# A hybrid decoder block on one core: the convolution branch's projection by seven quarter products instead of eight, with block sums of its operands kept in DRAM

## The chip, the cores and the metric

One core of a Trainium2 chip runs the whole kernel. The time is device microseconds of one execution; a kernel's time is the median of several. The kernel before has 1921.81 us (three runs, 1920.85 to 1922.24).

## The reference, cut to what matters

One layer, 2048 tokens, 1024 channels, everything in float32. The change concerns `y_a`, and the order of work around it.

```python
h = rms_norm(x, norm_g)
u = jnp.einsum('bsd,dc->bsc', h, w_in)
v_c, b_c, c_c, z_c, q, k, v, z_a, gate_logits = jnp.split(u, SPLIT_POINTS, axis=-1)

y_c = b_c * causal_depthwise_conv(c_c * v_c, conv_w)
y_c = y_c * jax.nn.silu(z_c)
y_a = jnp.einsum('bsc,cd->bsd', y_c, w_conv_out)
...
o = sliding_window_attention(q, k, v, sinks) * jax.nn.silu(z_a)
y_b = jnp.einsum('bsc,cd->bsd', o, w_attn_out)

gates = jax.nn.sigmoid(gate_logits + gate_b)
g_a, g_b = jnp.split(gates, N_BRANCHES, axis=-1)
merged = g_a * y_a + g_b * y_b
return x + jnp.einsum('bsd,de->bse', merged, w_out)
```

## The kernel before

**Tiling.** The tokens are worked on in two sets of T = 1024 (`t` = 0 and 1). A projection is computed in *units*: 256 output columns (two blocks of 128, index `i`) by the 1024 tokens of the set (two halves of H = 512, index `q`). The reduction over 1024 channels has 8 chunks of 128 (KC = 8), as 4 pairs (KP = 4): a pair index `j` and a parity `p`. Each float32 product is made of three matmuls of rounded parts: high by high, high by low, low by high. So a chunk takes 3 matmuls, and a plain unit 4 quarters x 8 chunks x 3 = 96 matmuls of 128x512.

**Seven quarter products.** `sunit` (L443 to L476) computes a unit by a scheme of the Strassen and Winograd kind: output blocks `i` and token halves `q` are the quarters of the result, parities `p` those of the reduction, and seven products of quarter size (`product`, L426) on sums and differences of quarters take the place of eight. A product is 4 chunks x 3 = 12 matmuls, a unit 84. Operands are numbered 1 to 8: 1, 2, 8 and 3 are the raw quarters, 5, 6, 7 and 4 sums of them; `op_split` makes the high part (ScalarE) and the low part (VectorE) of one. The weights' sums are made per unit: one by an accumulating DMA on GpSimd's queue (`added`, L269), three by VectorE (L363). `qunit` (L478) computes a unit by plain products from the raw quarters alone.

**Order.** `run` (L623) drives everything by a clock of products: at each tick (12 matmuls) it takes one step of the unit's generator, issues weight loads ahead (`ahead_loads`), one piece of weight preparation (`piece`, L387), and what was `put` to that tick. So the order on each engine's queue is written out by hand in ticks. Per set: q, conv and gate units, z units of the convolution branch (`z`) and of attention (`za`), then four `yb` units (attention's projection), then four `ya` units (the convolution's projection); after both sets eight `o` units. In the second set k, v come first, then one `ga` unit at its place after them. Attention's blocks are put to a list of ticks between the units.

**The stage that is changed.** The gated convolution is written to DRAM (`ocd`) in the z stage. During `yb` it is read back in 16 tiles of 128x512 a set (`load`, names `ocr`), split by `split_op` into `opa`, and `ya_unit` (L1248) computes its units by `branch` and `mm_t` (L1167), 8 chunks for each of 4 quarters. The result is multiplied by the gate (read back from `gd` into one of two buffers of `upool`, named `tha`, L1256) and accumulated into `mt` in DRAM by GpSimd's queue (L1262); `yb`'s results have been written to `mt` before. During `ya`, `next_tile` (L1568) reads the second set's rows of x (whole rows, 512 KB) and columns of x transposed (`h`) on ScalarE's queue, computes the norm and makes the operands of the next set; after the second set `wo_side` (L1287) does the like for `w_out`. Weights for `ya` are laid out by the host in another form (`branch` in `_layout`, kind "T" in `pieces_of`): two halves of 4 chunks each.

Of the kernel before, what the change touches and what calls it, by code (L numbers as in the profile page):

```python
# [15 lines left out]
P = 128  # L16
# [40 lines left out]
EARLY = (1, 0)  # L57
# [6 lines left out]
def block_kernel(  # L64
# [56 lines left out]
    yd = [dram.tile([KC, P, T], F32, name=f"yd{t}") for t in range(NT)]  # L121
    mt = [dram.tile([KC, P, T], F32, name=f"mt{t}") for t in range(NT)]
# [153 lines left out]
    def load_half(i=None):  # L276
# [12 lines left out]
        if kind == "R":  # L289
            raw = both[:, h]  # L290
            for p in range(2):
                nc.sync.dma_start(raw[:, p], srcs[(2 * h + p) * P : (2 * h + p + 1) * P])

                for c in FIRST_X.get((i, p), ()):
                    xt_load(c, 0)
        elif kind in "SP":
            raw = both.rearrange("p k h (j c) -> p k h j c", c=P)
            for k in range(2) if key[0] == "o" else (slice(0, 2),):
                nc.sync.dma_start(raw[:, k, h], block_of(n, h, k))
            if kind == "S" and h:  # L300
                put(tick[0] + ADDED, lambda: added(n))
        else:
            raw = both[:, h].rearrange("p k (j c) -> p (k j) c", c=UC)
            w, c0 = srcs
            nc.sync.dma_start(raw, w[c0 // UC, h].rearrange("r (j c) -> r j c", c=UC))
# [12 lines left out]
    def pieces_of(n):  # L318
# [52 lines left out]
        def part(p):  # L371
            hi, lo = (v.rearrange("p (j c) -> p j c", c=UC) for v in wpair(f"{name}_{p}"))
            w[p] = (hi, lo)
            return two(hi, lo, raws[2 * n + p])

        return w, [(2, 0, lambda: part(0)), (2, 2, lambda: part(1))]
# [10 lines left out]
    def piece():  # L387
# [4 lines left out]
        need = [2 * n + i] if plan[n][0] in "TP" else [2 * n, 2 * n + 1][: 1 + min(i, 1)]  # L392
# [717 lines left out]
    def fin_g(t, w, j):  # L1110
        def fin(i, q, val):
            k = 2 * j + i
            th = slot([P, H], F32, f"th{t}_{w}_{k}_{q}")
# [45 lines left out]
    def split_op(src, name):  # L1159
        o = optile(name)  # L1160
        split(o[:, 0], o[:, 1], src)
        return o


    YA_CHUNKS = (0, 2, 4, 6, 1, 3, 5, 7)

    def mm_t(ps, u, half, opt, q, last):  # L1167
        cs = slice(half * P, (half + 1) * P)
        for n, k in enumerate(YA_CHUNKS):
            j, p = divmod(k, 2)  # L1170
            force(u, p)
            hi, lo = ready[u][p]
            o = opt[k, q]
            for i, (w, m) in enumerate(((hi, 0), (hi, 1), (lo, 0))):
                nc.tensor.matmul(  # L1175
                    ps, lhsT=w[:, j, cs], rhs=o[:, m, :],
                    start=n == 0 and i == 0, stop=n == KC - 1 and i == 2)
            if n == KP - 1:
                live[0] -= 2 * last
                yield  # L1180
        live[0] -= 2 * last

    def quarters(order):
        return [(hf, q) for q in order for hf in range(2)]

    def branch(t, key, j, opt, fin, order):
        u = unit((key, t, j))
        for n, (hf, q) in enumerate(quarters(order)):
            ps = bank(f"{key}{t}_{j}_{hf}_{q}")
            yield from mm_t(ps, u, hf, opt, q, n == 3)  # L1190
            fin(2 * j + hf, q, ps)
            yield

    def load(src, k, q, name):
        tl = slot([P, H], F32, name)
        nc.sync.dma_start(tl, src[k, :, hs(q)])
        return tl

# [27 lines left out]
    def yb_unit(t, j, ops):  # L1226
        th = {}
        order = ((0, 1), (1, 1), (0, 0), (1, 0)) if j == 0 else ((0, 0), (1, 1), (0, 1), (1, 0))

        def get(n):  # L1230
            pair = upool.tile([P, 2 * H + 2], F32, tag="u", name=f"thb{t}_{j}_{n}")
            for e, (i, q) in enumerate(order[2 * n : 2 * n + 2]):
                th[i, q] = pair[:, hs(e)]
                nc.sync.dma_start(th[i, q], gd[t][1][2 * j + i, :, hs(q)])

        def fin(i, q, val):
# [7 lines left out]
            nc.sync.dma_start(mt[t][2 * j + i, :, hs(q)], m)  # L1244

        return yb_first(t, ops, fin) if j == 0 else sunit(("yb", t, j), ops, fin), get

    def ya_unit(t, j, opt, order):  # L1248
        th = {}

        def get(n):
            pair = upool.tile([P, 2 * H + 2], F32, tag="u", name=f"tha{t}_{j}_{n}")
            for i, (hf, q) in enumerate(quarters(order)[2 * n : 2 * n + 2]):
                k = 2 * j + hf
                th[k, q] = pair[:, hs(i)]
                nc.sync.dma_start(th[k, q], gd[t][0][k, :, hs(q)])  # L1256

        def fin(k, q, ps):
            m = th[k, q]
            vec.scalar_tensor_tensor(  # L1260
                out=m, in0=m, scalar=1.0, in1=ps, op0=ALU.add, op1=ALU.mult)
            nc.gpsimd.dma_start(mt[t][k, :, hs(q)], m, accum_op=ALU.add)  # L1262

        return branch(t, "ya", j, opt, fin, order), get
# [3 lines left out]
    def fin_o(n):  # L1268
# [4 lines left out]

        def get(i, q):
            xr = xrs[i, q] = slot([P, H], F32, f"xr{n}_{i}_{q}")
# [11 lines left out]
    def wo_side(n0, st):  # L1287
        raw = st["raw"]

        def ld(c):  # L1290
            for q in range(2):
                h = raw[c, q] = slot([P, H], F32, f"wo_{c}_{q}")
                nc.scalar.dma_start(h, w_o[c * P : (c + 1) * P, hs(q)])

        def sums(j):
            a, b = 2 * j, 2 * j + 1
            sub(raw[a, 1], raw[b, 1], raw[a, 1])
            sub(raw[a, 0], raw[b, 1], raw[a, 0])

        for j in range(KP):  # L1300
            for i in range(2):
                put(n0 + 2 * j + i, lambda c=2 * j + i: ld(c))
            put(n0 + 6 + 2 * j, lambda j=j: form(2, 1, j, st))
            put(n0 + 7 + 2 * j, lambda j=j: sub(raw[2 * j, 0], raw[2 * j, 1], raw[2 * j, 0]))
            put(n0 + 8 + 2 * j, lambda j=j: form(2, 5, j, st))
            put(n0 + 9 + 2 * j, lambda j=j: sums(j))
            put(n0 + 17 + j, lambda j=j: form(2, 6, j, st))
            put(n0 + 28 + j, lambda j=j: form(2, 2, j, st))
            put(n0 + 30 + j, lambda j=j: form(2, 7, j, st))
            put(n0 + 22 + j, lambda j=j: last_sum(j, st))  # L1310
            put(n0 + 32 + j // 2, lambda j=j: form(2, 3, j, st))
            put(n0 + 34 + j // 2, lambda j=j: form(2, 4, j, st))
# [3 lines left out]
    for t in range(NT):  # L1316
# [9 lines left out]
        else:  # L1326
            at_(("k", t), COL_K)
            at_(("v", t), COL_VV)
        for j in range(EARLY[t]):
# [16 lines left out]
        for j in range(NJ):  # L1346
            plan.append(("T", (w_co, j * UC), ("ya", t, j)))
    for n in range(S // P // 2):
        t, c0 = divmod(2 * n * P, T)
        s(("o", n), (mt[t], c0), (mt[t], c0 + P))  # L1350

# [216 lines left out]
    def next_tile(t, n0):  # L1568

        st = x_state(t)  # L1570
        raw, ops, xs = st["raw"], st["ops"], st["x"]

        def ld(b):
            xs[b] = x_load(t, b, nc.scalar)

        def stats(b0):
            ss = st["ss"][b0] = small.tile([P, 2], F32, tag="sx", bufs=4, name=f"ss{t}_{b0}")
# [187 lines left out]
```

## Time and profile before

| | |
|---|---|
| median of 3 runs | 1921.81 us (1920.85 to 1922.24) |
| profiled execution | 1922.65 us, its span 1920.9 us |
| granted TensorE clock | 1.000 |
| matmuls | 8774, of these 7894 of 128x512 |
| TensorE / VectorE / ScalarE / GpSimd busy | 1908.7 / 1454.0 / 973.0 / 606.9 us |
| data moved | 378.87 MB, 197 GB/s on average |
| `ya` stage of the first set | about 804.7 to 892 us |
| `ya` stage of the second set | 1677.5 to 1764.5 us |

The profile is of one execution; its times start with the span. In a group of instructions, `out<-in` gives the program's names, then the shape, the count after x, and after the bar the busy time, the mean time of one in ns, and the idle time of the engine ahead of them. SPq and POOLq are the queues of the engines that issue DMAs. In the waits, the name to the right of the arrow is what ended the wait.

### The profile page before, as it was taken

The page shows a single profiled execution, that of the slowest core. Times are in us where ns is not written, and L with a number is a line of the kernel's source. Part 1 is how long each engine was busy: PE and PEld are TensorE (multiplying, and loading weights), DVE is VectorE, ACT ScalarE, POOL GpSimd, SP SyncE. Part 2 cuts the span into 40 slices and gives each one's busy share as a digit, 9 for nine tenths or more (in the row PEclk, how much of TensorE's full clock was granted, in tenths as well). Part 3 has the DMA queues.
Part 4 walks back from the last instruction along what each step waited for, and adds up shares of the span by engine and source line. Part 5 has one row for each costly group of instructions (what it writes and reads, how often), then busy time and mean ns, then how long its engine had stood idle before and what let it go on. Part 6 is the DMA issues. An engine that isn't in the chain of part 4 may idle for free.

```text
span 1920.9 us, 27491 instructions
## 1 busy us (share of the span) xinstructions
PE 1908.7 (99%) x8774; PEld 1589.1 (83%) x8774; DVE 1454.0 (76%) x2501; ACT 973.0 (51%) x1935; POOL 606.9 (32%) x833
## 2 busy tenths in 40 slices
PE   8999999999999999999999999999999999999999
PEld 7888888888888888888888888888888888888887
DVE  7988888888777659668688888878888458755544
ACT  7555455456666344334565554556666335423221
POOL 2043435446564100011432444546665000011000
PEclk9999999999999999999999999999999999999999
DMA  8298556668887544894696665678887624886663
GB/s 298 86 238 211 168 168 185 181 195 257 243 267 236 171 121 152 297 285 104 165 229 172 186 174 157 179 232 243 245 256 228 200 98 144 271 233 137 175 191 110
DMA packets 278928, 378.87 MB, mean 197 GB/s; under 512 B 62784, under 2 KB 141632, under 8 KB 278784
## 3 DMA queue, kind: packets, MB, share of 16 engines
q1 hardware_dynamic: 233216, 280.57, 46.5%
q0 software_dynamic: 39664, 83.92, 19.8%
q10 hardware_dynamic: 5904, 12.62, 2.0%
q8 instruction: 70, 1.15, 0.3%
q14 instruction: 74, 0.61, 0.1%
HBM read 263.49 MB, written 113.51 MB: 196 GB/s over the span
## 4 chain that ended last, share of the span: by engine, by line
PE 96%; DMA 2%; DVE 1%; ACT 0%; POOL 0%; issue 0%; SPq 0%; DVEq 0%; POOLq 0%; ACTq 0%
PE Y L432 33%; PE ya L1175 9%; PE Vcv L432 5%; PE Xcv L432 4%; PE po L1037 2%; PE Vgb L432 2%; PE Xgb L432 2%; PE Xz L432 2%; PE Vo L432 2%; PE Xo L432 2%; PE Vza L432 2%; PE Xza L432 2%; PE yb L1216 2%; PE Vb L432 2%; PE Vz L432 2%; PE Xb L432 2%
## 5 line engine op out<-in xcount | busy, mean ns | idle before, releaser
L999 POOL DMA_DIRECT2D x<-fd x256 | 141.4, 565 | 116.1 <-DMA fd<-f 68.0
L972 ACT ACTIVATE p<-s,st,rq 128x128 f32<-128x128 f32 x256 | 113.0, 451 | 0.8 <-DMA fd<-f 0.6
L1020 POOL TENSOR_SCALAR_AFFINE_SELECT xh<-xh 64x512 fp32r<-64x512 f32 x64 | 64.7, 1011 | 106.2 <-DVE xl L214 79.6
L1262 POOL DMA_DIRECT2D mt<-tha x32 | 27.8, 881 | 217.3 <-DVE tha L214 195.3
L992 POOL DMA_DIRECT2D fd<-f x64 | 39.6, 618 | 152.4 <-DVE f L214 135.4
L432 PE MATMUL Xcv<-oph,wcv_ah 128*128 128x512 f32 x256 | 79.2, 390 | 0.0
L1175 PE MATMUL ya<-opa,wya_0h 128*128 128x512 f32 x256 | 79.0, 390 | 0.0
L1175 PE MATMUL ya<-opa,wya_1h 128*128 128x512 f32 x256 | 78.8, 389 | 0.0
L214 DVE SCALAR_TENSOR_TENSOR tha<-tha,ya 128x512 f32<-128x512 f32 x32 | 22.0, 686 | 61.1 <-PE ya L1175 55.8
L1020 POOL TENSOR_SCALAR_AFFINE_SELECT xl<-xl 64x512 fp32r<-64x512 f32 x64 | 60.5, 946 | 4.4
L1020 POOL TENSOR_SCALAR_AFFINE_SELECT yp<-yp 64x512 fp32r<-64x512 f32 x64 | 58.8, 919 | 4.2
L1020 POOL TENSOR_SCALAR_AFFINE_SELECT yp<-xl 64x512 fp32r<-64x512 f32 x64 | 57.8, 904 | 3.1
L214 DVE TENSOR_TENSOR o<-po,o 64x256 f32<-64x256 f32 x128 | 53.5, 418 | 5.2 <-ACT o L1049 4.3
L1175 PEld LDWEIGHTS ya<-opa,wya_1h 128*128 128x128 f32 x256 | 48.0, 188 | 9.9
L1175 PEld LDWEIGHTS ya<-opa,wya_0h 128*128 128x128 f32 x256 | 47.9, 188 | 9.9
L432 PEld LDWEIGHTS Xcv<-oph,wcv_ah 128*128 128x128 f32 x256 | 47.6, 188 | 9.6
L274 POOL DMA_DIRECT2D wyb_raw<-in_w_attn_out x6 | 5.1, 842 | 156.3 <-DMA wyb_raw<-in_w_attn_out 74.5
L214 DVE SCALAR_TENSOR_TENSOR y<-u,cols,y 128x512 f32<-128x512 f32 x64 | 49.9, 779 | 3.5 <-ACT y L1086 2.3
L1049 ACT COPY o<-po 64x256 f32<-64x256 f32 x128 | 47.1, 368 | 10.1 <-PE po L1037 4.7
L972 ACT ACTIVATION_READ_ACCUMULATOR p<-s,st,rq 128x1 f32 x256 | 50.9, 199 | 0.0
L214 DVE TENSOR_TENSOR p<-p,st 128x512 f32<-128x512 f32 x64 | 48.1, 752 | 3.4 <-DMA q<-q2d 0.3
L214 DVE TENSOR_TENSOR ophc<-zain,ophc 128x512 fp32r<-128x512 f32 x64 | 42.2, 686 | 11.1 <-ACT ophc L241 11.1
(628 smaller groups left out, 6384.0 us busy)
## 6 DMA issues: line engine op xcount, KB each, us to landing
gd<-th SPq DMA_DIRECT2D x64, 256.0 KB, 3.3
wcv_raw<-in_w_in SPq DMA_DIRECT2D x32, 512.0 KB, 5.3
q<-q2d SPq DMA_DIRECT2D x64, 256.0 KB, 5.3
v<-vd SPq DMA_DIRECT2D x128, 128.0 KB, 4.0
fd<-f POOLq DMA_DIRECT2D x64, 256.0 KB, 4.6
x<-fd POOLq DMA_DIRECT2D x256, 64.0 KB, 3.7
wga_raw<-in_w_in SPq DMA_DIRECT2D x16, 512.0 KB, 5.6
wq_raw<-in_w_in SPq DMA_DIRECT2D x16, 512.0 KB, 6.0
```

What stands on the lines that cost most here:

```text
L214: r = f(*args, **kw)
L274: nc.gpsimd.dma_start(raw[:, 0, 1], block_of(n, 1, 1), accum_op=ALU.add)
L432: nc.tensor.matmul(ps, lhsT=w[:, j, :], rhs=b[:, m, :], start=start and j == 0 and i == 0, stop=j == KP - 1 and i == 2, skip_group_check=n ...
L972: nc.scalar.activation(out=p[:, i, :], in_=sg[:, i, HD : 3 * HD], func=AF.Exp, bias=st[:, 1, i : i + 1], scale=rv[:, i // 2, i % 2 : i % 2 ...
L992: nc.gpsimd.dma_start(fd, f)
L999: nc.gpsimd.dma_start(x[QUADS[k]], src[k])
L1020: nc.gpsimd.affine_select(out=d4, in_=s4, pattern=[[0, 2], [-32 * sg, 2], [0, G], [-sg, 32]], compare_op=ALU.is_gt if prev else ALU.is_ge, ...
L1037: nc.tensor.matmul(po[:, cs], lhsT=v2[:, kind, :], rhs=xx[:, :, h * HD : (h + 1) * HD], start=n == 0, stop=n == 2)
L1049: nc.scalar.copy(ov, pov[oth, :, e])
L1175: nc.tensor.matmul(ps, lhsT=w[:, j, cs], rhs=o[:, m, :], start=n == 0 and i == 0, stop=n == KC - 1 and i == 2)
L1216: nc.tensor.matmul(banks[i, q], lhsT=w[:, j, :], rhs=b[:, l, :], start=n == 0 and m == 0, stop=n == KC - 1 and m == 2, skip_group_check=True)
L1262: nc.gpsimd.dma_start(mt[t][k, :, hs(q)], m, accum_op=ALU.add)
```

## The change

1. **`ya` by seven products.** `y_unit` replaces `yb_unit` and `ya_unit`. The first unit of each set's `ya` is plain (`qunit`), the other three are `sunit`s. `w_conv_out` is laid out as the other weights are, so the "T" form, `mm_t`, `branch`, `load` and `split_op` go. Gate halves and the accumulation into `mt` stay as they were.
2. **Block sums by way of DRAM.** In the last `z` unit of the convolution branch `csum` reads the four quarters of `ocd` per pair `j` into slots (16 loads a set), makes four differences on VectorE, and writes them to a DRAM tensor `csd`. The operands of `ya` (32 a set, instead of 16) are read by `conv_op` from `ocd` (raw quarters) or `csd` (sums), three ticks ahead of the split, at ticks of a table (`CONV_AT`).
3. **First units plain.** The second set runs its first two `ga` units ahead of k and v, the first of them plain; the first `o` unit is plain.
4. **Queues and places.** The columns `h`, the rows of x (now as halves of 256 KB, 16 loads) and `w_out` are loaded by SP instead of ScalarE's queue, and from the `yb` stage on; the squares work on 512 columns at a time. Attention's ticks, and those of the next set's operands, are given by tables. Attention of the second set ends later, in the z stage.

Instructions before and after: matmuls 8774 and 8726; DMAs issued by SP 1264 and 1408, by ScalarE 41 and 1, by GpSimd 563 and 567; activation table loads 8 and 10.

```diff
-EARLY = (1, 0)
+EARLY = (1, 2)
+CSUM_AT = ((3, 3, 11, 15), (1, 6, 13, 12))
+CONV_AT = ((5, 2, 4, 3, 6, 2, 5, 6, 6, 6, 5, 6, 7, 7, 12, 12, 12, 12, 11, 13, 14, 14, 14, 16, 15, 17, 12, 16, 17, 19, 20, 19), (3, 1, 1, 1, 1, 1, 4, 7, 5, 4, 8, 6, 8, 8, 7, 9, 12, 12, 13, 14, 14, 15, 15, 10, 14, 16, 18, 18, 19, 20, 19, 17))
...
+    csd = [dram.tile([4, KP, P, H], F32, name=f"csd{t}") for t in range(NT)]
...
-        nc.scalar.dma_start(h, xt2[c * P : (c + 1) * P, t * T + q * H : t * T + (q + 1) * H])
+        nc.sync.dma_start(h, xt2[c * P : (c + 1) * P, t * T + q * H : t * T + (q + 1) * H])
...
-    def yb_unit(t, j, ops):
+    def y_unit(t, w, j, ops):
...
-            nc.sync.dma_start(mt[t][2 * j + i, :, hs(q)], m)
-
-        return yb_first(t, ops, fin) if j == 0 else sunit(("yb", t, j), ops, fin), get
-
-    def ya_unit(t, j, opt, order):
...
-        return branch(t, "ya", j, opt, fin, order), get
+            to = mt[t][2 * j + i, :, hs(q)]
+            if w:
+                nc.sync.dma_start(to, m)
+            else:
+                nc.gpsimd.dma_start(to, m, accum_op=ALU.add)
+
+        if j:
+            return sunit(key, ops, fin), get
+        return (yb_first(t, ops, fin) if w else qunit(key, ops, fin)), get
...
-            plan.append(("T", (w_co, j * UC), ("ya", t, j)))
+            s(("ya", t, j), (w_co, j * UC), (w_co, j * UC + P))
+            if j == 0:
+                plan[-1] = ("P",) + plan[-1][1:]
...
+        if n == 0:
+            plan[-1] = ("P",) + plan[-1][1:]
...
+        def csum(n, j):
+            raw, to = {}, csd[t]
+
+            def ld():
+                for i in range(2):
+                    for q in range(2):
+                        o = raw[i, q] = slot([P, H], F32, f"cr{t}_{j}_{i}_{q}")
+                        nc.sync.dma_start(o, ocd[t][2 * j + i, :, hs(q)])
+
+            def out(m, a, b, c):
+                sub(a, b, c)
+                nc.sync.dma_start(to[m, j], a)
+
+            put(n, ld)
+            put(n + 2, lambda: out(0, raw[0, 0], raw[0, 1], raw[0, 0]))
+            put(n + 3, lambda: out(1, raw[0, 1], raw[1, 1], raw[0, 1]))
+            put(n + 4, lambda: out(2, raw[1, 1], raw[1, 1], raw[0, 0]))
+            put(n + 5, lambda: out(3, raw[1, 0], raw[1, 0], raw[1, 1]))
...
-        n1 = n0 + KC + 7 * (NJ - 2)
-        for n, (k, q) in enumerate((k, q) for q in range(2) for k in YA_CHUNKS):
-            def oc_load(k=k, q=q):
-                yc[k, q] = load(ocd[t], k, q, f"ocr{t}_{k}_{q}")
...
-            put(n1 - 11 + n, oc_load)
-            put(n1 + 2 + n // 2, oc_form)
...
+        b0 = n0 + KC + 7 * (NJ - 2)
+
+        def conv_op(n, m, j):
+            src = {8: (0, 1), 1: (0, 0), 2: (1, 0), 3: (1, 1)}.get(m)
+            got = slot([P, H], F32, f"oc{t}_{m}_{j}")
+            if src:
+                nc.sync.dma_start(got, ocd[t][2 * j + src[0], :, hs(src[1])])
+            else:
+                nc.sync.dma_start(got, csd[t][(5, 7, 6, 4).index(m), j])
+            put(n, lambda: op_split(f"y{t}", m, j, got, conv["ops"]))
+
+        for i, (m, j) in enumerate((m, j) for m in (1, 2, 8, 3, 5, 6, 7, 4) for j in range(KP)):
+            n = b0 + CONV_AT[t][i]
+            put(n - 3, lambda n=n, m=m, j=j: conv_op(n, m, j))
...
-        run(sunit(("o", n), state[NT]["ops"], fin))
+        run((sunit if n else qunit)(("o", n), state[NT]["ops"], fin))
```

More of the change, by code (lines that the diff above doesn't have):

```diff
@@ L369, in pieces_of @@
                        (2, 0, lambda: of_sums(0, 6, 5, "s")), (2, 2, lambda: of_sums(1, 3, 7, "t"))]
[L371 to L376, printed above, removed]
+        assert False, kind
     def open_prep():
@@ L391, in piece @@
         n, i, cost, last, f = todo[0]
[L392 removed]
+        need = [2 * n + i] if plan[n][0] == "P" else [2 * n, 2 * n + 1][: 1 + min(i, 1)]
         if live[0] + cost > WRING or any(k not in raws for k in need):
@@ L1157, in fin_z @@
         return fin, load
[L1159 to L1197, printed above, removed]
     def yb_first(t, ops, fin):
@@ new lines, in square, with norm @@
+        def square(b):
+            q, i = divmod(b, HB)
+            if i == 0:
+                ss[q] = small.tile([P, HB, 2], F32, tag="sx", bufs=4, name=f"ss{t}_{q}")
+            junk = ps_s.tile([P, 2, H], F32, tag="s", name=f"xsq{t}_{b}")
+            for h in range(2):
+                nc.scalar.activation(
+                    out=junk[:, h], in_=st["x"][b, h], func=AF.Square, accum_out=ss[q][:, i, h : h + 1])
+        def norm(q):
+            rt[q] = small.tile([P, HB], F32, tag="sr", bufs=2, name=f"rt{t}_{q}")
+            both = small.tile([P, HB], F32, tag="sm", name=f"sb{t}_{q}")
+            add(both, ss[q][:, :, 0], ss[q][:, :, 1])
+            seen_[q] = x_rsqrt(t, q * HB, HB, both, rt[q])
```

200 lines of the change are left out of this document (89 added, 111 removed).

## The prediction

> **What bounds the kernel now.** I read the page's busy times and chain first, then the chain in order of time, the waits of TensorE, and the windows of the stages that the change touches.
>
> ```profile
> span 1920.9 us, 27491 instructions
> PE 1908.7 (99%) x8774; PEld 1589.1 (83%) x8774; DVE 1454.0 (76%) x2501; ACT 973.0 (51%) x1935; POOL 606.9 (32%) x833
> PE 96%; DMA 2%; DVE 1%; ACT 0%; POOL 0%; issue 0%; SPq 0%; DVEq 0%; POOLq 0%; ACTq 0%
> ```
>
> TensorE is busy in 1908.7 of 1920.9 us and holds 96% of the chain that ended last. A busy matmul engine alone would prove little, so I look at pieces of that chain (start us, length us, what):
>
> ```profile
> 54.52 21.76 PE Qga L492 x96
> ...
> 1598.59 21.76 PE yb L1216 x96
> ...
> 1677.49 87.04 PE ya L1175 x384
> ...
> 1914.13 2.73 PE Y L432 x12
> ```
>
> Four different stages run at one pace: 21.76 / 96 = 87.04 / 384 = 0.22667 us per matmul of 128x512, and the last product of a `sunit` has 2.73 us for 12. The 384 matmuls of the second set's whole `ya` stage stand as one unbroken piece. So in these stages matmuls, issued back to back, set the end, and a matmul taken out there takes 0.22667 us off the path as long as nothing else becomes late. What TensorE ever waits for is short (us in total, times, longest):
>
> ```profile
> PE ptr L556 <- DVE rtok L550: 2.5, 1, 2.5
> PE Y L1375 <- DVE zero L133: 1.5, 1, 1.5
> PE ptq L647 <- DVE k_l L214: 1.2, 1, 1.2
> PE kv L512 <- ACT wkv0h L241: 1.0, 1, 1.0
> PE s L943 <- DMA v<-vd: 0.8, 1, 0.8
> PE Y L432 <- ACT Y L450: 0.7, 1, 0.7
> ```
>
> The first four belong to the start-up, which the change leaves as it is. The last two sum to 1.5 us. There is little waiting for a new order to win back.
>
> **The change, part by part.** The sum is made against the profiled execution: 1922.65 us, a span of 1920.9, and 0.84 us above the median of 1921.81.
>
> *Matmuls.* A `ya` unit had 96 matmuls (four quarters of 8 chunks times 3); by `sunit` it has 7 products of 12, so 84. Three of four units in each of two sets change: 2 x 3 x 12 = 72 fewer, 72 x 0.22667 = **-16.32 us**. The first unit of each `ya` stays at 96. Two units that were `sunit`s become plain: the second set's first `ga` unit and the first `o` unit, 2 x 12 x 0.22667 = **+5.44 us**. Matmuls 8774 become 8726. Net **-10.88 us**.
>
> *VectorE and ScalarE.* Durations of the operations added (busy us, mean ns):
>
> ```profile
> L214 DVE TENSOR_TENSOR opa<-ocr,opa 128x512 fp32r<-128x512 f32 x32 | 20.5, 686 | 9.5 <-ACT opa L241 9.5
> L241 ACT CAST opa<-ocr 128x512 fp32r<-128x512 f32 x32 | 17.7, 618 | 0.0
> L214 DVE TENSOR_TENSOR wya_1l<-wya_raw,wya_1h 128x1024 fp32r<-128x1024 f32 x8 | 9.7, 1219 | 0.0
> L214 DVE TENSOR_TENSOR wo_raw<-wo_raw 128x512 f32<-128x512 f32 x24 | 15.8, 687 | 0.3
> ```
>
> The 32 block subtractions of `csum` are 32 x 0.687 = 22.0. Splits of operands go from 88 to 128: 40 x 0.686 = 27.4. The `ya` weights were 16 splits of 128x1024; they become 22 of these, 6 of 128x512, and 18 block sums: 6 x 1.219 + 24 x 0.687 = 23.8. Six more `sunit`s with two additions each: 8.2. Two units made plain save about 10. In all some +71 us of VectorE, 4% of the span, with 1920.9 - 1454.0 = 467 us idle. ScalarE gains the high halves, 40 x 0.618 = 24.7, less than it has idle several times over. What counts is the stage (us, then busy us of PE, PEld, DVE, ACT, POOL, granted clock, DMA share, GB/s):
>
> ```profile
> 725.80:804.70 78.90, 78.90 (x349) 65.31 (x349) 62.70 (x92) 38.15 (x59) 1.70 (x2) 1.00 0.66 216
> 768.00:816.00 48.00, 48.00 (x213) 39.74 (x213) 30.99 (x44) 18.23 (x28) 0.86 (x1) 1.00 0.88 297
> 804.70:892.68 87.98, 87.98 (x394) 72.86 (x393) 63.30 (x134) 27.88 (x44) 14.57 (x17) 1.00 0.84 234
> 816.00:864.00 48.00, 48.00 (x218) 39.74 (x217) 29.19 (x83) 17.06 (x28) 8.58 (x10) 1.00 0.99 284
> 1598.50:1677.50 79.00, 79.00 (x350) 65.41 (x349) 62.78 (x93) 38.20 (x59) 1.67 (x2) 1.00 0.65 213
> 1677.50:1764.50 87.00, 87.00 (x385) 72.03 (x385) 45.83 (x66) 17.87 (x26) 15.22 (x17) 1.00 0.78 193
> ```
>
> The `yb` and `ya` stages of the first set (rows 1 and 3) leave VectorE idle in 16.2 and 24.7 us, those of the second (rows 5 and 6) in 16.2 and 41.2. By the same durations, the operations that fall into each stage after the change come to 4 us more in the first set's `yb`, 3 more in its `ya`, which also gets 8 us shorter, 1 more in the second `yb` and 12 more in its `ya`. About 13 us of idle VectorE remain in the tightest of them. The eight table rows of 128x512 that were one 128x1024 square, and the two sets' `csum`, lie under `z` products where VectorE has a like margin. Cost: **0**, hidden under TensorE. Without that cover the whole 71 us would show.
>
> *The activation tables.* In the second set attention now runs further into the `z` stage, so that exponentials stand between the gates' activations and two table loads are added, as the first set has them now:
>
> ```profile
> L1143 ACT ACT_TABLE_LOAD x4 | 5.1, 1283 | 2.1 <-issue 1.2 <-PE Xz L432 0.8
> ```
>
> Two are 2.57 us of ScalarE, which the copy of Y (L450) can be queued behind. Bounds: 0, if hidden, and 2.57, if TensorE waits through both. The nearest row is the first set's, where such a copy held TensorE for 0.7 us. I take **+0.7**. The Trainium skill ("ScalarE: Activation LUTs", What ACT_TABLE_LOAD costs) gives the same 1283 ns but adds a drain of about 1380 ns per switch. By its 2.66 us for each the upper bound would be 5.3 us and, scaled alike, the term 1.4. No row of the trace shows such a drain by itself.
>
> *Attention's places.* The lists of ticks for scores and values move. Between removing the 0.8 us wait above for v, with its surroundings, and adding one like it: -0.8 to +0.8, taken as **0**, since most of these places move by one to three products.
>
> *DMAs.* Issue to landing (KB, median us), and the spread of `ocr`:
>
> ```profile
> ocd<-zin SPq DMA_DIRECT2D x32, 256.0 KB, 3.0
> ...
> ocr<-ocd SPq DMA_DIRECT2D x32, 256.0 KB, 5.0
> wya_raw<-in_w_conv_out SPq DMA_DIRECT2D x16, 512.0 KB, 6.6
> ...
> mt<-tha POOLq DMA_DIRECT2D x32, 256.0 KB, 6.1
> ```
>
> ```profile
> DMA to landing us min/median/max: 2.7/5.0/7.8
> ```
>
> SP gets 144 more: 32 loads and 32 stores for `csum`, 32 more operand loads, and 48 that ACT issued before (16 h, 16 w_out, 16 half rows of x). All move 256 KB. The 96 new ones are 25 MB. In the `z` stage they cost nothing I can see: the written sums are read again more than 29 products (79 us) later. In the `ya` stage they matter. Of each set's 32 operand loads, 18 and 16 now fall behind the start of `ya`, where before none did: 18 x 0.262 = 4.7 MB. Three accumulating weight loads of 0.5 MB add 1.6, and the first set's x rows (4.2 MB) leave for `yb`. Row 3 carried 87.98 x 234 = 20.6 MB; it becomes about 22.7, over 79.8 us **285 GB/s**. Row 6 has 87.00 x 193 = 16.8 and becomes about 22.6 over 78.9, 286. Row 4 moved 284 GB/s at a DMA share of 0.99, row 2 297 at 0.88, and TensorE lost nothing in either. So the stage comes to about the highest rate that the trace shows. Each operand is loaded three products, 3 x 2.72 = 8.2 us, ahead of its split, against a longest landing of 7.8. Bounds: nothing, and, if row 4's 284 GB/s is the ceiling and the weights prefetched for the next stage (1.7 MB more, 24.4 in all) must pass too, 24.4 / 0.284 = 85.9 us for 79.8, so 6 us a set, 12 in all. I take **0**, by row 4, which ran 48 us at that share without a wait.
>
> The Trainium skill ("DMA: Bandwidth & Descriptors", Issuing engines are not separate DMA queues) speaks against hoping for anything from the move from ACT to SP: all issuers share the same 16 engines. Its specification of about 358 GB/s of HBM for one core would leave 20% of room at 285; row 4, at 0.99 with 284, says the room is smaller, and the measurement decides. By the page the term would be 0 without doubt.
>
> *Sum:* 1922.65 - 16.32 + 5.44 + 0.7 = 1912.5 for a profiled run, 0.84 less for a median: **1911.6 us**, 0.53% faster.
>
> **The rivals.**
>
> 1. *DMA is the bound of both `ya` stages.* For it: 285 GB/s wanted where 284 filled the engines. Against it: the operands come in the stage's first half, weights are loaded ahead, and the stage after has room for what is left over, at a share of 0.38:
>
> ```profile
> 892.68:934.00 41.32, 41.32 (x197) 34.17 (x197) 30.14 (x54) 21.38 (x37) 5.14 (x7) 1.00 0.38 88
> ```
>
> It gives 6 to 12 us of TensorE waiting in split operands (`oc`): 1917.6 to 1923.6, within 0.2% for the most part.
>
> 2. *SP's order makes it slower.* A load of a gate half (`th`) needs its buffer back, and SP holds everything behind it until the accumulation into `mt` has landed:
>
> ```profile
> SPq L1256 <- DMA mt<-tha: 101.6, 14, 9.6
> ```
>
> Mean 7.3 us, longest 9.6. Before, only weights far ahead stood behind it. Now operand loads due in three products do. Hold and landing together are 7.3 + 5.0 = 12.3 to 9.6 + 5.0 = 14.6 against 8.2 us of lead: 4.1 to 6.4 us late, at three holds while operands are loaded, in two sets: 25 to 38 us, so 1936 to 1950. It decides as soon as a hold is over 8.2 - 5.0 = 3.2 us. Against it: in the first, plain `ya` unit the accumulations of the first pair are issued in its second and fourth product, and with 6.1 us to land they are through about 3 us after the next gate load is reached in the seventh; holds before were long because the load was queued early. In part (one or two places) it would give 1916 to 1924.
>
> 3. *More is won.* The new places remove the waits in the second set's attention (0.8), the table loads hide (0.7), and of the 4.5 us that TensorE idles outside the waits above (1920.9 - 1908.7 - 7.7) two or three go: 1907 to 1909.
>
> 4. *The plain units and the weights do not keep up.* The first `sunit` of `ya` needs its 7 weight blocks one unit earlier than halves were needed. If its weight load (6.6 us median) and sums came a product late in each of six units, 6 x 2.72 = 16 us eat the gain: 1928. Weights are loaded two units ahead in `yb`, by the same scheme and with no wait there, which speaks against it.
>
> **How the numbers follow.** Forecast, 1909 to 1917.5: 0.62. Rival 3: 0.12. Rival 1, with the mild part of 2: 0.14. Rivals 2 and 4: 0.12. A measurement of this kernel tells about 0.2% (3.8 us) from no change, so faster means below 1918.0 and slower above 1925.7: faster 0.62 + 0.12 + 0.02 of rival 1 = 0.76, same 0.12, slower 0.12. The range leaves out the outer half of rival 3 and rivals 2 and 4: 1907.5 to 1923.
>
> **What would show it.** 8726 matmuls at 0.2267 us; chain pieces of `ya` units 19.0 us long instead of 21.76, one plain unit of 21.76 in each `ya` and at the head of `o`. VectorE near 1520 us busy, all stages below TensorE's time. If rival 1 holds: DMA share 0.99 and over 280 GB/s through `ya`, with TensorE waiting for `opy` of ACT or DVE and these for loads. If rival 2: the same waits with DMA share well below 0.9, and waits of SP for `mt<-` in front of `oc` loads. If rival 4: waits for `wya` sums. I am wrong if TensorE waits more than 6 us in the two `ya` stages, or if the second set's `z` shows waits of over 3 us behind table loads.

## The result and the profile after

The changed kernel takes **1935.36 us** (median of 4 runs, 1933.88 to 1936.6) against 1922.03 for the kernel before (4 runs): a ratio of 1.0069, 95% interval 1.0051 to 1.0086. The forecast was 1911.6. It is slower by 13 us.

The page of the changed kernel, the lines that answer to the first three shown of before:

```profile
span 1934.2 us, 27765 instructions
PE 1906.2 (99%) x8726; PEld 1582.1 (82%) x8726; DVE 1512.8 (78%) x2577; ACT 1010.2 (52%) x2009; POOL 616.1 (32%) x837
...
PE 70%; DMA 12%; DVE 8%; issue 4%; POOL 3%; ACT 2%; SPq 1%; DVEq 0%; POOLq 0%; ACTq 0%
```

The matmuls are 8726, as forecast, and VectorE has 59 us more (71 were forecast). But TensorE's busy time fell by 2.5 us where 10.9 were expected, and its idle time rose from 12.2 to 28.0 us: -10.9 + 8.4 + 15.8 = +13.3. Its share of the chain fell from 96% to 70%. What it waits for, the longest lines:

```profile
PE Y L432 <- ACT Y L450: 3.5, 4, 1.4
PE Vz L432 <- DVE wz_sl L223: 3.0, 1, 3.0
PE Y L432 <- DVE b L223: 2.8, 2, 2.4
PE Y L432 <- DVE s5ya L223: 2.5, 1, 2.5
...
PE s L943 <- DMA q<-q2d: 1.4, 1, 1.4
PE Vq L432 <- DVE wq_sl L223: 1.3, 1, 1.3
PE Qya L492 <- DVE th L223: 1.2, 1, 1.2
PE Y L432 <- DVE s5yb L223: 1.1, 1, 1.1
```

None of these is a line of the kernel before, but for `Y <- ACT Y` (0.7 there). They are spread over the kernel: `b` and `wz` are units of other projections. To see where the time goes I added up, by stretch, how much longer each matmul came after the one before it than the median for that pair of shapes (us; from the traces; the last six columns are experiments told below):

```
stretch, us  before  after | front_only front_mended first_old start_early ya_mended mended_early_oc
144 to 192     0.1    1.8  |    0.2        0.1          0.1       0.4         0.1        0.1
336 to 432     0.3    6.0  |    6.2        0.4          0.4       0.3         5.2        0.4
768 to 912     0.3    7.2  |    0.0        0.0          6.7       5.6         0.2        2.7
912 to 1248    2.3    3.2  |    2.3        3.9          2.0       7.9         2.0        4.1
1248 to 1440   2.4    3.9  |    3.3        2.8          3.1       3.6         2.0        2.9
1440 to 1488   0.1    6.1  |    6.0        0.1          7.4       0.2         5.9        0.1
1680 to 1824  -0.2    2.8  |   -0.2       -0.2          3.6       3.2         0.5        1.9
whole kernel  16.9   41.0  |   29.3       19.6         36.5      31.9        27.1       22.9
```

41.0 - 16.9 = 24.1 us of waiting, and 24.1 - 10.9 = 13.2: the difference is accounted for. Less than half of it (768 to 912 and 1680 to 1824: 10 us) lies in `yb`, `ya` and `o`. Most of the rest (11.7 us) lies in two stretches where attention's blocks run: around 410 us, and around 1475 us in the second set's z stage.

A part is the clock. The windows of the changed kernel around its wait at 409 us (PE busy third, granted clock third from the end; x is the count of matmuls):

```profile
408.00:412.00 4.00, 1.64 (x8) 1.02 (x7) 3.90 (x7) 0.00 (x0) 2.86 (x5) 1.00 0.65 136
412.00:416.00 4.00, 4.00 (x12) 3.13 (x13) 3.92 (x8) 2.39 (x3) 0.58 (x2) 0.64 0.84 251
```

After 2.4 us without a matmul the next 12 took 4 us instead of 2.7, at a granted clock of 0.64.

### The profile page after: what moved, and what is told of

Read it like the earlier page. It is cut to its first block, busy times and chain, and to the rows that moved or that the text cites. A ratio compares the mean times of both kernels' runs of the same rounds, so it can differ in the third digit from the quotient of the medians.

```text
span 1934.2 us, 27765 instructions
## 1 busy us (share of the span) xinstructions
PE 1906.2 (99%) x8726; PEld 1582.1 (82%) x8726; DVE 1512.8 (78%) x2577; ACT 1010.2 (52%) x2009; POOL 616.1 (32%) x837
## 4 chain that ended last, share of the span: by engine, by line
PE 70%; DMA 12%; DVE 8%; issue 4%; POOL 3%; ACT 2%; SPq 1%; DVEq 0%; POOLq 0%; ACTq 0%
PE Y L432 27%; PE Xcv L432 4%; PE Vcv L432 4%; PE Vza L432 2%; PE Xza L432 2%; PE Qga L492 2%; DMA q2d<-q_l 2%; PE Xgb L432 2%; PE Xb L432 2%; PE Vo L432 2%; PE po L1037 2%; DMA fd<-f 2%; PE Xo L432 2%; PE Vga L432 2%; PE Vgb L432 2%
## 5 line engine op out<-in xcount | busy, mean ns | idle before, releaser
L1020 POOL TENSOR_SCALAR_AFFINE_SELECT yp<-xl 64x512 fp32r<-64x512 f32 x64 | 62.6, 978 | 3.1
L250 ACT CAST ophy<-oc 128x512 fp32r<-128x512 f32 x64 | 38.4, 621 | 38.0 <-DMA oc<-ocd 21.0
L1221 POOL DMA_DIRECT2D mt<-th x32 | 28.4, 887 | 87.8 <-DVE th L223 79.8
L223 DVE TENSOR_TENSOR ophy<-oc,ophy 128x512 fp32r<-128x512 f32 x64 | 42.1, 687 | 17.3 <-ACT ophy L250 17.2
L223 DVE TENSOR_TENSOR p<-p,st 128x512 f32<-128x512 f32 x64 | 52.8, 825 | 3.2 <-PE Xz L432 0.2
L250 ACT CAST ophc<-zain 128x512 fp32r<-128x512 f32 x64 | 37.2, 619 | 26.0 <-DVE zain L223 26.0
L794 POOL DMA_DIRECT2D q2d<-q_h x64 | 46.4, 915 | 10.4 <-issue 6.2
L283 POOL DMA_DIRECT2D wq_raw<-in_w_in x8 | 7.3, 918 | 132.3 <-DMA wq_raw<-in_w_in 39.4
L223 DVE TENSOR_TENSOR xl<-x,xh 128x512 fp32r<-128x512 f32 x64 | 43.7, 683 | 6.0 <-DMA fd<-f 4.0
L223 DVE STREAM_TRANSPOSE f<-p 128x512 f32<-128x512 f32 x64 | 45.5, 711 | 3.1 <-DMA kq<-q2d 0.2
```

The lines of the kernel that those rows point to most:

```text
L223: r = f(*args, **kw)
L250: nc.scalar.copy(hi, src)
L794: eng.dma_start(q2d[t][j][half, q * 2 * HB : (q + 1) * 2 * HB, i, e, :], src[HALVES[e]].bitcast(F32).rearrange("p (b x) -> p b x", x=HD))
L1020: nc.gpsimd.affine_select(out=d4, in_=s4, pattern=[[0, 2], [-32 * sg, 2], [0, G], [-sg, 32]], compare_op=ALU.is_gt if prev else ALU.is_ge, ...
L1221: nc.gpsimd.dma_start(to, m, accum_op=ALU.add)
```

## The experiments

Theories. **A1**: the new places of attention and the new order at the head of the second set block the queues. **A2/D**: bytes; the added and moved loads fill the DMA engines (my rival 1). **C**: loads asked for too late hold a queue (near my rival 2). **A3**: `csum`. Each ratio is to the kernel before, on the same chip. `places0` is the first set's old list of ticks.

**The changed kernel again**, no edit.

> The changed kernel itself, for a second profile of it. If its 24 us of added waiting are fixed by the order of its instructions (theory A: queues written out by hand block each other), the time is 1933 to 1937 and TensorE waits at the same places again, with sums within 3 us: near 145, 409, 788 to 800, 872, 1023, 1404, 1475 and 1703 us. If they are accidents of when DMAs land (theory B), the sum stays near 41 us but half of these places change.

1933.45 us, 1.0056 (1.0041 to 1.0071). The places at 145, 411, 798, 871, 1470 and 1699 us return, with 38.9 us in all; those at 788, 1023 and 1404 do not. So the loss is mostly one of order, which is the same in both, with some accidents.

**Only the front of the change.**

```diff
 # kernel before
-EARLY = (1, 0)
+EARLY = (1, 2)   # both by sunit, ahead of k and v
+STEPS = (the changed first list, the changed second list, one tick less)
 ...               # gate halves of those ga units: in wide tiles of upool, as in the changed kernel
```

> The kernel before with only the new order at the head of the second set (two ga units ahead of k and v, both by seven products) and the new places of attention; ya, its operands, csum, the queues of the loads are those of before. Matmuls 8774 as before. Theory A1 (the new order and the new places of attention are what makes TensorE wait, some 15 us outside of yb and ya): 1932 to 1938. Theory A2 (the loads that the change adds or moves are the cause, in yb, ya and the z stage): 1920 to 1925.

1935.03 us, 1.0058 (1.0038 to 1.0077), with not one matmul fewer or more and no byte added. Its waits stand at 336 to 432 and 1440 to 1488 us, as in the changed kernel, and there are none in `yb` and `ya`. **A1 holds**, and is as large as the whole net loss of the changed kernel: the seven-product `ya` with its loads gains about what it loses.

**Old places in the changed kernel.**

> The changed kernel with the places of attention of before: the first set's list as it was, the second set's moved by 15 ticks (the units now ahead of q) in its first half and by 10 in its second. Theory A1: the waits near 350 to 416 us go and those of the second set change, 1923 to 1929. Theory A2: 1932 to 1937, since attention's places do not matter.

```diff
-STEPS = (...)
+STEPS = (places0, (66, 72, 76, ..., 129, 135, 139, 139, 142, ..., 191, 194))
```

1962.96 us, 1.0207 (1.0192 to 1.0222): a miss. The first set's waits went (336 to 432 us: 0.3), but my second list put two blocks on one tick and let attention run 11 ticks into z: 25 us from 1248 to 1392, 16 from 1440 to 1584. That attention's places decide is plain; by how much was not to be had from this run.

**No `csum`.**

> The changed kernel without csum: no loads of quarters, no differences, no stores to csd in the last z unit; the operands 5, 6, 7 and 4 of ya are read from raw quarters of ocd instead, in the same number and size, so the values of y_a are not the reference's. If csum's 64 DMAs and 32 subtractions cost something in the z stages (theory A3), the waits near 590 to 621 and 1469 to 1483 us go: 1928 to 1931. Theories A1 and that of the ya stage's loads alone: 1934 to 1937.

```diff
-                    csum(tick[0] + CSUM_AT[t][i], i)
+                    pass
...
-                nc.sync.dma_start(got, csd[t][(5, 7, 6, 4).index(m), j])
+                nc.sync.dma_start(got, ocd[t][2 * j + ...])     # a raw quarter in place of the sum
```

1934.24 us, 1.006 (1.0045 to 1.0075); 7.0 us near 1475, as in the changed kernel (6.1). A3 falls: making the block sums and writing them to DRAM costs nothing that can be measured. The operands of `ya` are read here in the same number and size.

**The first set's old places alone**, and **one number of them.**

> The changed kernel with the first set's places of attention as before, the second set's as changed. Theory A1 (two blocks of attention two ticks apart, 102 and 104 where they were 99 and 104, pile up on VectorE and make TensorE wait 2.5 us, and the clock then falls to half for some 3 us): the waits of 336 to 432 us (4.5 to 6 us in two profiles) go and nothing else changes, 1927.5 to 1930. The rival (the same work only collides elsewhere): 1932 to 1936.

> The changed kernel with one number different: the ninth block of the first set's attention at tick 99, as before, instead of 102 (its neighbour stays at 104). If this one place makes the pile-up of 336 to 432 us (4.5 to 6 us), those waits go and the time is 1928 to 1931, like that of the run with the whole old list. If it takes several of the moved places: 1932 to 1936.

```diff
-STEPS = ((60, ..., 95, 102, 104, ...), ...)
+STEPS = (places0, ...)                          # c2_first_old
+STEPS = ((60, ..., 95, 99, 104, ...), ...)      # c3_one_place
```

1930.09 us, 1.0039 (1.0026 to 1.0052), and 1932.02, 1.0051 (1.0034 to 1.0067). The old list removes 5.6 us of waiting from 336 to 432 us (4.1 against the second profile of the changed kernel), the one number 2.8 (1.3): TensorE still waits 2.0 us at 409 us with it. So the pair 102, 104 of my theory is not the cause of that wait; its two blocks have their scores at about 311 and 320 us, long before. The block that runs there is the fifteenth, put to tick 129 instead of 130. VectorE in the kernel before (start, length, instruction, then idle before it):

```profile
393.87 0.06 DVE L214 MEMSET u<- 128x2 f32 x1
395.88 0.43 DVE L214 COPY_PREDICATED s<-mask_i,s 128x256 f32<-128x256 int32 x1 [1.19 <-PE s L947]
405.40 0.68 DVE L214 TENSOR_TENSOR b<-Y,s5b 128x512 f32<-128x512 f32 x1
```

and in the changed kernel:

```profile
398.26 0.42 DVE L223 COPY_PREDICATED s<-mask_i,s 128x256 f32<-128x256 int32 x1
400.80 0.06 DVE L223 MEMSET u<- 128x2 f32 x1
401.65 1.54 DVE L223 SCALAR_TENSOR_TENSOR y<-u,cols,y 128x512 f32<-128x512 f32 x2 [0.79 <-ACT y L1086]
405.49 0.16 DVE L223 TENSOR_TENSOR st<-st 128x4 f32<-128x4 f32 x1 [0.94 <-ACT p L972]
411.21 0.68 DVE L223 TENSOR_TENSOR b<-Y,s5b 128x512 f32<-128x512 f32 x1
```

TensorE needs the addition `b` to have read Y before it may write Y again. One tick earlier, the block's scores (the masking of `s`) run ahead of the zeroing of `u`, on which the convolution's `y` depends. ScalarE waits for it:

```profile
ACT y L1086 <- DVE u L223: 5.0, 1, 5.0
```

VectorE in turn stands for that `y`, and then for the softmax's output `p`, and `b` starts 4.5 us after Y is complete instead of 0.7. The scores run ahead of `u` in all seven profiles that have this wait, and behind it in three that have not (before, `first_old`, `start_early`). No run moved this block alone, so that its one tick is the cause is what the traces suggest and not shown. VectorE is no fuller there than without the wait: from 384 to 412 us it is busy for 24.9 of 28 us, in `first_old` for 26.0. It is the order that differs.

**The second set's last 16 blocks one to four ticks earlier**, as well.

> The kernel of the run before this one, and the last 16 blocks of the second set's attention moved forward by one tick at first and four at the end (140, 143 to 185 instead of 141, 145 to 189), so that attention ends in z where it did before. Theory A1: of the 6 to 6.5 us lost near 1470 us most goes, 1922 to 1925. Rival: the blocks then collide in the units of b and ga instead, as the run with the old places showed it there at 1248 to 1344 us with another list: over 1928.

```diff
-138, 141, 145, 148, ..., 185, 189))
+138, 140, 143, 146, ..., 182, 185))
```

1936.23 us, 1.0072 (1.0053 to 1.0092): a miss. 6.5 us stay near 1470, and 9 appear from 1296 to 1440. Nearness to z was not the cause. What stands in the way, in this kernel from 1440 to 1475 us (total, times, longest):

```profile
ACT p L972 <- DMA fd<-f: 7.5, 2, 7.1
DVE st L223 <- ACT p L972: 6.7, 2, 6.5
...
PE Y L432 <- DVE zs L223: 3.2, 1, 3.2
```

A block's softmax writes its output `p` to a buffer that held `f` of an earlier block, and must wait until that one's store to `fd` in DRAM has landed (7.0 us after it was issued); VectorE stands behind the softmax, and the next z unit's sum `zs` behind that. In the changed kernel it is VectorE's `xl` that waits 4.0 us for the buffer of such a store, with the weights' sum `wz_sl` behind it. The stores took about as long before (6.3 to 7.1 us), when the blocks stood 3.5 ticks apart; my reading is that 3 ticks (8.2 us) leave them too little room, which the next run tests.

**More room instead**: start earlier, old spacing; or **one ga unit ahead of k and v** instead of two.

> The changed kernel with the first set's old places, and the second set's attention begun 8 ticks earlier (58 instead of 66), so that its last 16 blocks stand three and a half ticks apart, as before, and end at 185. Theory E (two ga units ahead of k and v leave attention 14 ticks less room before z; its blocks, 3 ticks apart, queue behind their own round trips through DRAM): of the 9 to 10 us lost from 1300 to 1490 us under 3 remain, 1922 to 1926. Theory F (the z stage itself has become the obstacle, by csum or by the loads): the 6 to 7 us near 1470 stay, 1928 to 1932.

> The changed kernel with the first set's old places and one ga unit ahead of k and v in the second set instead of two; attention begins at 59, with the spacing of before up to tick 136, and ends at 185. Matmuls as in the changed kernel. Theory E: waits of 1300 to 1490 us under 5 us, 1923 to 1928. Theory F: 1928 to 1932.

```diff
+STEPS = (places0, (58, 63, 67, ..., 129, 133, 136, 140, ..., 182, 185))   # c3_start_early
+EARLY = (1, 1); STEPS = (places0, (59, 65, ..., 136, 138, 141, 144, 146, ...))   # c3_one_ahead
```

1931.48 us, 1.004 (1.0025 to 1.0054), and 1938.2, 1.0077 (1.0058 to 1.0095). In the first the waits near 1475 us are gone (7.4 to 0.2): theory E stands at that place, though the time lies in the range of its rival F. For 4.8 us appear at 1067 to 1095 in attention's first blocks, 1.5 of them scores that wait for the low part of k to be loaded. In the second the 1475 wait is gone too, and my list, 2 or 3 ticks apart around 140, put 12 us at 1296 to 1392 in its place; the time misses both ranges.

**Bytes or order in `yb` and `ya`.**

> The changed kernel with attention as changed, and three moves around ya, none of which removes a byte: the squares of the next set's rows two ticks later, the norms of the columns that followed their load by only two or three ticks later, and the gate half for the first ya unit one tick earlier. Theory C (the 6 to 8.5 us of waiting in yb and ya are instructions that hold their engine's queue for a DMA that was asked for too late): they fall to under 3 us, 1928 to 1931. Theory D (my rival 1: the DMA engines are full there, at 284 to 318 GB/s): the waits come back at the next instruction, 1932 to 1936.

> The changed kernel with the first set's old places; of each half row of x for the second set's statistics only 32 of 512 columns are loaded and squared, so the root mean square of that set is not the reference's. This takes 3.9 MB out of yb and ya of the first set, and leaves every instruction in its place. Theory D (bytes: the DMA engines are full there): the waits of 768 to 890 us (6.7 us in the run with the old places of the first set alone) fall to under 3 us, 1925 to 1928. Theory C (instructions that hold a queue for a DMA asked for too late, in part other than these): 1928 to 1931.

```diff
+ROWS_AT = (..., 5, 7, 8, 9, 10, 11, 10, 11, 10, 13, 28, 28)        # c2_ya_moves: squares, norms + 2
+COL_AT = (32, 34, 35, 39, 39, 39, 39, 37, 35, 34, 33, 31, ...)
+put(tick[0] + (6 if n == NJ - 1 else 7 if n % NJ else 5), ...)
...
+nc.sync.dma_start(x[:, 0:32], ...)                                  # c3_short_rows, on places0
```

1934.27 us, 1.0063 (1.0046 to 1.008), and 1927.62, 1.0028 (1.0015 to 1.0042; the run it builds on has 1.0039). Both times lie in theory D's ranges, so the waits must decide. Without 3.9 MB of rows the wait in `yb` is gone (2.0 to 0), but others grew, and 768 to 912 has 6.6 us after 6.7, where D had under 3; the time fell by some 2 us (the intervals overlap), and shorter squares go with the shorter rows. From 768 to 816 us this kernel moved 278 GB/s instead of 340, and the operands landed no sooner (6.4 us median after 6.2). The moves removed the wait at 872 and brought others: 2.1 us in `yb`, where VectorE stood for a high half that ScalarE made only after the squares, and 1.7 in the second `ya`. That waits come back at the next instruction is what D foresaw; the run `ya_mended` below parts the two. What stood on VectorE at 872 us in the changed kernel, where TensorE waited 2.5 us for `s5ya`:

```profile
873.38 0.75 DVE L223 SCALAR_TENSOR_TENSOR h<-h,cols,rb 128x512 f32<-128x512 f32 x1 [3.22 <-DMA h<-in_xt]
874.04 0.68 DVE L223 TENSOR_TENSOR wya_d<-wya_raw,wya_d 128x512 fp32r<-128x512 f32 x1
874.65 0.68 DVE L223 TENSOR_TENSOR s5ya<-Y,s5ya 128x512 f32<-128x512 f32 x1
```

The norm of a column, due only dozens of products later, held VectorE for its load; the sum that TensorE needs stood two behind it. The column's load was due three ticks (8.2 us) ahead and landed in 6.2 us, but SP issued it 8.2 us after its tick (the time of a tick is my estimate, from the count of matmuls). SP's queue, and what it waited for:

```profile
859.90 0.80 SPq L1207 DMA_DIRECT2D th<-gd  x2
865.87 1.20 SPq L308 DMA_DIRECT2D wga_raw<-in_w_in  x2
867.11 1.07 SPq L581 DMA_DIRECT2D h<-in_xt  x2
...
SPq L1207 <- DMA mt<-th: 7.5, 1, 7.5
SPq L308 <- DVE wya_tl L223: 5.1, 1, 5.1
```

A gate half (`th`) had to wait for its buffer, until the accumulation into `mt` had landed, and a load of weights for its own; the column came behind both. That is my rival 2.

**All moves together, first try.**

> Both places of attention and the three moves of the run before this one together. If theories A1 and C hold and add up: 1933.5 - 5.5 - 5 - 5 = 1918, so 1915 to 1921, and faster than the kernel before. If the moves collide: over 1924.

1933.22 us, 1.0057 (1.004 to 1.0074): a miss. It holds the denser list of the second set, and waits where `both_places` did (8.8 us from 1248 to 1440, 4.7 from 1440 to 1488).

**The mended places together**, then the operands one tick earlier, then another start.

> The changed kernel with the first set's old places; the second set's attention begun at 64 with its last 16 blocks 3.5 ticks apart; the norms of the columns later after their loads; the statistics of the rows three ticks later; the gate half of the first ya unit one tick earlier. If the whole loss is a matter of places (theories E and C add up): the waits near 1470, 864 and 1699 us are gone, with 3 to 8 us left in attention's first blocks, ya and o; 1918 to 1924. If each move only shifts a wait to the next instruction: 1927 or more.

> The kernel of the run before this one, with the operands of ya loaded four ticks ahead of their split instead of three. If what is left near 819 and 829 us is their late landing: 1.5 to 3 us less than that run. If the loads then wait for slots or hold SP: the same or more.

> The mended kernel with the second set's attention begun at 62 instead of 64. If the waits of 1050 to 1100 us of the run that began at 58 come from scores asked for before k and q are back from DRAM, a start at 62 has them smaller or not at all: within 2 us of the mended kernel.

```diff
+STEPS = (places0, (64, 68, 73, ..., 125, 129, 133, 136, 140, ..., 182, 185))
+COL_AT, gate half: as in c2_ya_moves; ROWS_AT: squares as changed, norms + 3
-            put(n - 3, lambda n=n, m=m, j=j: conv_op(n, m, j))
+            put(n - 4, lambda n=n, m=m, j=j: conv_op(n, m, j))      # c4_mended_early_oc alone
```

1925.22 us, 1.0011 (0.9998 to 1.0024); **1917.71**, 0.9977 (0.9968 to 0.9986), faster than both kernels; and 1926.17, 1.0017. The first fell between its two ranges. The one tick of lead is worth 7.5 us, where I expected 1.5 to 3; of 8.7 us less waiting in the profiles 5.3 lie from 768 to 912 us. Landing of these loads (us, min, median, max) in the changed kernel:

```profile
DMA to landing us min/median/max: 3.7/6.3/8.5
```

Three ticks are 8.2 us; the kernel before had 2.7/5.0/7.8 for its loads from `ocd`. The waits of the mended kernel with three ticks, 815 to 830 us:

```profile
ACT ophy L250 <- DMA oc<-ocd: 7.8, 2, 6.3
DVE ophy L223 <- ACT ophy L250: 6.7, 4, 4.8
...
PE Qya L492 <- ACT ophy L250: 2.7, 2, 2.1
```

Late landing alone does not explain them, as the first of these loads landed in 6.6 us. SP in the mended kernel, with its wait:

```profile
811.13 0.43 SPq L1672 DMA_DIRECT2D oc<-csd  x1
815.25 0.80 SPq L1207 DMA_DIRECT2D th<-gd  x2
816.10 0.90 SPq L1670 DMA_DIRECT2D oc<-ocd  x2
...
SPq L1207 <- DMA mt<-th: 7.5, 3, 3.6
```

and with the fourth tick:

```profile
811.16 1.04 SPq L1670 DMA_DIRECT2D oc<-ocd  x2
812.25 1.43 SPq L1672 DMA_DIRECT2D oc<-csd  x3
814.70 1.02 SPq L1207 DMA_DIRECT2D th<-gd  x2
```

With three ticks five operand loads are due at about 811.6 us (the same estimate), behind a gate half that waits for `mt`, and go out 4.4 to 7.1 us late. With four the five go out ahead of it. They land no sooner for that (3.0/6.5/10.1 us, after 3.6/6.6/8.8). Here the tick gets round a hold of SP's queue.

**The parts apart, and a fifth tick.**

> The kernel before with the new order at the head of the second set, as in the run of that alone (1935.0 us), but with the first set's old places of attention and the second set's blocks begun at 63 and 3.5 ticks apart at the end. If the loss of that run is the places and not the order of the units: 1922 to 1926, within 4 us of before. If two ga units ahead of k and v cost by themselves: 1929 or more.

> The changed kernel with attention's places as changed, and all moves around ya: norms and statistics later, the gate half of the first ya unit one tick earlier, operands loaded four ticks ahead. If loads asked for too late were the whole loss in yb and ya: the waits of 768 to 912 and of 1680 to 1776 us fall from 9 to 11 us to under 5, and the time to 1926 to 1930; the waits near 409 and 1470 us stay. If that part is bytes: 1932 to 1936.

> The fastest kernel so far (1917.7 us) with the operands of ya loaded five ticks ahead of their split instead of four. If their lead still costs something there: up to 1.5 us less. If four cover the landing (longest 10.1 us, four ticks are 10.9) and a fifth only holds slots: the same within 1.5 us, or more.

```diff
+front_only with STEPS = (places0, (63, 67, ..., 181, 184))      # c5_front_mended
+the changed kernel with the ROWS_AT, COL_AT, gate half and n - 4 above   # c5_ya_mended
+c4_mended_early_oc with n - 5                                    # c5_lead_5
```

1925.84 us, 1.0014 (1.0004 to 1.0023); 1926.58, 1.0016 (1.0007 to 1.0026); 1918.1, 0.9967 (0.9953 to 0.9982). So the order of the units costs little by itself (2.7 us), and the places cost 8.5 (1.0058 to 1.0014). In `ya_mended` the waits of `yb` and `ya` are gone, 10.0 to 0.7 us, with the same loads; the end of its first `yb` and its first `ya` (DMA share and GB/s last):

```profile
768.00:816.00 48.00, 48.00 (x212) 39.44 (x211) 35.18 (x74) 30.47 (x60) 1.69 (x2) 1.00 1.00 356
816.00:864.00 48.00, 48.00 (x217) 39.84 (x216) 35.13 (x51) 20.94 (x32) 8.01 (x10) 1.00 1.03 308
```

356 GB/s at a share of 1.00, 308 at 1.03, and TensorE never idle. **Bytes were not the bound**, and the 284 GB/s that the prediction took for about the highest rate are not the ceiling either. A fifth tick changes nothing that can be measured.

## Why the prediction was wrong, point by point

- *Matmuls, -10.88 us*: right; 8726, and the fastest kernel, with the same ones, has 22.9 - 16.9 = 6.0 us more waiting than before, hence -4.9 by sum and -4.4 by ratio.
- *VectorE's +71 us at nothing, hidden under TensorE*: 59 us were measured, and they are hidden: `ya_mended` has all this work in its place and 0.7 us of waiting in `yb` and `ya`. But busy sums of whole stages could not show what did cost time: one instruction some 4 us late (409 us), or behind a waiting one (872, 1475). That belongs to the next two terms.
- ***Attention's places*, "-0.8 to +0.8, taken as 0, since most of these places move by one to three products": this step failed.** It measured about +11 us (`front_only`, with the order of units and wide tiles for its gate halves); 8.5 of them go with other places. The size of a shift says nothing of what it costs: in the first set the traces point to one block that moved by a single tick and came ahead of an instruction that others wait for. In the second, 3.5 ticks became 3 for sixteen blocks, because two units were put ahead of them, and their buffers were not free in time.
- ***DMAs*, "I take 0, by row 4": this step failed too, by 8 to 10 us** (ratio 1.0056 to 1.0069 for the changed kernel, 1.0016 with its loads moved). It lay within my bounds of 0 to 12, but not for rival 1's reason, since TensorE lost nothing at 356 GB/s. What failed is the lead of 8.2 us against a longest landing of 7.8: it was counted from the tick to which a load is put, and SP's queue reached operand loads of the changed kernel up to 5.7 us later, a column 8.2. Landings grew as well, but less (median 5.0 to 6.3 us for the operands), and no run shows what made them grow.
- *Rival 2* was the nearest, in the mild part to which I had given 1916 to 1924 together with rival 1: SP stood 27.4 us, in eight waits, for `mt<-th` from 770 to 895 us, and what TensorE needed soon came behind. Before it stood 57.9 us there for the like, with nothing due soon behind it. Its sign of a DMA share well below 0.9 did not come (0.94 and 1.02 from 768 to 816 and 816 to 864 us). I did not foresee that VectorE and ScalarE are then held in turn, by an instruction that waits for such a load. *Rivals 3 and 4* did not show.
- *Activation tables, +0.7*: the two loads are there, at 1479.9 and 1489.7 us, after the wait at 1475 began; moving attention out of z took them away (`both_places`) and left the wait. After the first of them TensorE waits 0.7 us for the copy of Y that follows the softmax, which would fit the term, but no run isolates it. Their price stays open, and so does the wait at 145 us, which came in both profiles of the changed kernel and not in those of `no_csum` and `first_old`, which have the same instructions up to there.
- *The chances*: slower had 0.12. The two terms that I took as 0 had far more room to lose than to win, and I let them stand at the better end.

## What to carry to other kernels

In a kernel that runs by a hand-written order, cost a moved instruction by what stands directly before and behind it on its queue and by its distance to its neighbours, not by how far it moved or how idle its engine is on average. Count the lead of a load from when its queue really issues it, not from its place in the program: look for what stands ahead of it there and waits for a buffer. An instruction that is due much later must not stand in a queue waiting for its load. A change that cuts the work of the bounding engine by half a per cent can be lost twice over in this way, and be had back by moving a few ticks (1935.4 to 1917.7 us).

## What the runs showed of the hardware

Waits of TensorE that last 2.1 us or more are often, though not always, followed by up to nine matmuls of 128x512 at about twice their time (0.43 instead of 0.227 us), while the profile records a clock of 0.50 for 3.41 us. In the changed kernel's two profiles this came after 2.4 us at 409 and 3.0 at 1475 in the first, and after 3.5 at 1470 and 2.4 at 1699 in the second, but not after 2.5 at 872 in the first, nor after 2.3 at 411 in the second. The granted clock of the changed kernel's whole span was 0.996 to 0.998 in its four runs, by estimate some 4 to 8 us. The Trainium skill ("TensorE: Matmul & The Clock Gate", What's actually happening) tells of windows of about 3.4 us that run freely, after an idle one of which the clock is halved; that the place in such a window decides would fit with equal waits ending differently, but waits of 2.1 us, shorter than a window, were enough here (at about 800 us in `ya_moves` and in the run of all moves, and at 823 us in `c4_mended`). Why some waits are followed by it and others of the same length are not stays open.
